# Seven quarter products for eight in the first FFN product of two half layers of a decoder step

## The chip, the cores and the metric

The kernel runs on one core of a Trainium2 chip. The metric is the device time of one execution in microseconds (us); lower is better. The core's engines are PE (TensorE, the matmuls), DVE (VectorE), ACT (ScalarE), POOL (GpSimd, which here only issues DMAs) and SP (SyncE, which issues DMAs). Each engine works through its own list of instructions in order and waits on semaphores; the lists are fixed when the program is built.

## The reference

One step of a two-layer decoder: a retention layer, then a layer with windowed attention, each followed by a feed-forward network (FFN), with a norm before and after each part. 1024 tokens of a prompt and 32 of samples go through together, D = 1024 wide, the FFN 4096 wide. What matters here is the FFN, whose square makes a plain float32 product necessary:

```python
def ffn(h, g_pre, w1, w2, g_post):
    u = jax.nn.relu(rms_norm(h, g_pre) @ w1)
    return h + rms_norm((u * u) @ w2, g_post)
```

## The kernel before

The tokens are cut into half 0 (512) and half 1 (512 and the 32 samples, 544). Activations lie with the model dimension on the 128 partitions, so a token is a column. Every float32 product is made of three products of a reduced type: a number is cut into a high part `hi` and a rest `lo`, and `passes` lists hi x hi, hi x lo and lo x hi.

The FFN runs once for each half and layer: f0 (half 0, layer 0, its first product up to 1174 us in the profile, its second to 1353), f1 (half 1, layer 0), fa (half 0, layer 1) and f2 (half 1, layer 1, from 2489 us to the end). `Ffn.up(i)` (line 739) does 256 of the 4096 columns of W1, which is called a block here: `load_w` (310) loads two tiles of 512 KB by SP into `wraw` (line 318, two buffers), ACT casts the high part (`whi`, 328), DVE subtracts for the low part (`wlo`, 329), `proj_fm` (350) does the matmuls (line 356): for each of two groups of 128 columns eight steps along D, three passes, and one piece of 512 tokens (half 0) or two of 272 (half 1). ACT applies relu and square (748, 749), and POOL stores the block to HBM (`uD`, line 751). `ups` runs the blocks, `downs` the second product with `uD` fetched back by POOL (756).

The work between the products (norms, attention, transposes) is written as generators, called sides. `tick` (174) lets the present side take a step each time the matmuls have earned one, at a rate from the table `RATES` (156); `drain` takes all steps that are left. A scheduler then orders all instructions for each engine by the order of the text and the buffers. The sides named here are `norms` (281) with its statistic in `norm_r` (251: squares on ACT, sums on DVE, then two matmuls against ones, lines 265 and 266); "f0", the norm of half 1 beside f0's first product; "at1", "smp", "wo1" and "lt1", half 1's attention, its output product and the norm after it, all beside fa's second product; "at0", "wo0" and "lt0", the same for half 0 beside f1's; and "fo", the last norm, stores and transposes of half 0's output, beside f2's first product. Tiles called `x4` (146) are 8.5 KB in each partition; there are 13. PSUM has eight banks, four `mm` and four `aux`.

Of the kernel before, what the change touches and what calls it, by code (L numbers as in the profile page):

```python
# [116 lines left out]
def body(ctx, tc,  # L117
# [11 lines left out]
    def f32(ap):  # L129
        return ap.bitcast(F32)  # L130
# [30 lines left out]
    def side(gen, rate=None):  # L161
        sides.append((gen, rate))
# [88 lines left out]
    def norm_r(get, w):  # L251
# [19 lines left out]
        V.scalar_tensor_tensor(out=t, in0=t, scalar=3.0, in1=y0, op0=ALU.subtract, op1=ALU.mult)  # L271
        return t

    def xs_alloc():
        hi, lo = [x4(), x4()], [x4(), x4()]
        return [(hi[k // 4][:, k % 4], lo[k // 4][:, k % 4]) for k in range(KT)]
# [70 lines left out]
    def passes(a, b):  # L347
        return [(a[0], b[0]), (a[0], b[1]), (a[1], b[0])]
# [383 lines left out]
    class Ffn:  # L732
# [6 lines left out]
        def up(self, i):  # L739
# [10 lines left out]
            s_ = 2 * (i % 2)  # L750
            G.dma_start(out=uD[self.half][:, 2 * i:2 * i + 2], in_=self.st[:, s_:s_ + 2, :t_])  # L751

        def fetch(self, j):
            hi, lo = x4(), x4()
            t_ = TT[self.half]
            G.dma_start(out=f32(lo)[:, :, :t_], in_=uD[self.half][:, 4 * j:4 * j + 4])
            self.parts[j] = (hi, lo)

        def cut(self, j):
            t_ = TT[self.half]  # L760
            hi, lo = (t[:, :, :t_] for t in self.parts[j])
# [450 lines left out]
            S.activation(out=sel[:, i], in_=sel[:, i], func=AF.Copy, scale=den[:, i:i + 1])  # L1212

    def swa_sides(sw, half, am=None, skr=None):
        xs = []

        def late():
            xs.extend(xs_alloc())
            yield from norms(half, sw.y, g_spost, xs=xs, pre=g_f1)

        side(sw.attend(), f"at{half}")
        if half:
            side(sw.attend_sample(am, skr), "smp")
        side(sw.wo(), f"wo{half}")
        side(late(), f"lt{half}")
        return xs

    CHUNKS = [1, 2, 2, 2, 1]
    with tc.tile_pool(name="rp", bufs=1) as rp:
        G.dma_start(out=g_first, in_=gsrcs[0].rearrange("(k p) -> p k", p=P))  # L1230
# [4 lines left out]
        rets = [Ret(0, [(hi[k // 4][:, k % 4], lo[k // 4][:, k % 4]) for k in range(KT)], rp), None]  # L1235
        for _ in range(RATES["w0"]):
            next(ini)
        first = rets[0].qk_w(0, 0)
        run(ini)
        for g in (gen, x_store(0, loads), x_store(1)):  # L1240
            side(g, "x")
        qk = rets[0].qk(0, [[(0, 256)], [(256, 256)]], first)
        drain()
        prev = None
        for half in range(2):
            r = rets[half]
            for h in range(RH):
                pace[0] = RATES["vg"][half]
                last = h == RH - 1
                vs = r.v(h)  # L1250
                if last:
                    drain()
                    prev[0].wout(*prev[1:])
                    prev = None
                    xs = xs_alloc()
                    norm = norms(1 - half, xs=xs, pre=g_f0 if half else g_rpre)
                    side(norm, "n1")
                sg = r.g(h)
                while sides and (not last or sides[0][0] is norm):
                    advance()  # L1260
                og = (x4(), x4())
                side(r.core(h, qk, vs, sg, og))
                pace[0] = RATES["core"][half]
                if prev is not None:
                    prev[0].wout(*prev[1:])
                if prev is not None and prev[1] == RH - 1:
                    side(norms(0, prev[0].y, g_rpost), "rp")
                prev = (r, h, og)
                if not last:
                    qk = r.qk(h + 1)  # L1270
                elif half == 0:
                    rets[1] = Ret(1, xs, rp)
                    qk = rets[1].qk(0)
                else:
                    f0 = Ffn(0, 0, xs)
                    pace[0] = RATES["cl"]
                    for i in range(3):
                        f0.up(i)
        drain()
        prev[0].wout(*prev[1:])  # L1280
    with tc.tile_pool(name="sp", bufs=1) as sp:
# [56 lines left out]
        finish(f2, hT)  # L1338
# [31 lines left out]
```

## Time and profile before

| what | us |
|---|---|
| median of 3 runs (2905.68 to 2906.97) | 2906.42 |
| the profiled execution | 2905.74 |
| its span (first to last instruction) | 2903.9 |
| PE busy | 2849.2 (98%) |
| DVE busy | 1526.7 (53%) |
| ACT busy | 1264.1 (44%) |
| f0, blocks 5 to 15 of the first product | 123.1 |
| f2, blocks 2 to 15 of the first product | 172.4 |

PE is the engine that the others serve, and an average over the span hides where it waits. So the time of a stretch is read from the timeline of an engine that acts once in a block (POOL, with its store), and the waits from the rows on PE that have idle time before them. In such a row the start, the duration, the line and the tiles are followed by the idle time before it and what ended it.

### The profile page before, as it was taken

Reading aid. Unit: us, or ns where it says so; the run is one execution under the profiler, and the core shown is the slowest. Engines: PE = TensorE matmul, PEld = TensorE weight load, DVE = VectorE, ACT = ScalarE, POOL = GpSimd, SP = SyncE. Lnnn points to the kernel's source line nnn. Section 1 sums busy time; section 2 is a strip of 40 time slices with the busy share of each in tenths; the row PEclk is TensorE's granted clock in tenths of the full one; section 3 lists DMA queues with packets and bytes.
Section 4 is the critical chain, followed back from the end, with each engine's and each line's share of the span. In section 5 each row is a group of like instructions: output and inputs, shape, how many; then the busy total and the mean of one; then the engine's idle time right before and its main releaser. Section 6 shows DMA issues by size and latency. Waiting matters only on the chain.

```text
span 2903.9 us, 42531 instructions
## 1 busy us (share of the span) xinstructions
PE 2849.2 (98%) x16989; PEld 2487.6 (86%) x16989; DVE 1526.7 (53%) x3045; ACT 1264.1 (44%) x2554; POOL 177.3 (6%) x262
## 2 busy tenths in 40 slices
PE   8999999999999999999999999999999999899998
PEld 7888888888989788888998898978877788899998
DVE  5444565576566644553444664654357535542345
ACT  3343353343325444432545764445458533444322
POOL 2000000011010100000000000000010100000000
PEclk9999999999999999999999999999999999899999
DMA  6322332455263645553554333355432434346432
GB/s 206 93 83 89 95 113 87 157 169 176 91 209 97 219 144 173 179 152 98 163 165 131 126 96 95 109 164 163 156 128 87 131 94 150 105 148 217 157 103 68
DMA packets 418420, 391.08 MB, mean 135 GB/s; under 512 B 13878, under 2 KB 360286, under 8 KB 416174
## 3 DMA queue, kind: packets, MB, share of 16 engines
q1 hardware_dynamic: 380191, 248.97, 29.0%
q0 software_dynamic: 36848, 137.36, 13.3%
q8 instruction: 133, 2.18, 0.3%
q10 hardware_dynamic: 1183, 2.04, 0.2%
q14 instruction: 65, 0.53, 0.1%
HBM read 308.73 MB, written 79.56 MB: 134 GB/s over the span
## 4 chain that ended last, share of the span: by engine, by line
PE 88%; issue 4%; DVE 3%; DMA 2%; ACT 2%; POOL 0%; SPq 0%; DVEq 0%; ACTq 0%; POOLq 0%
PE mm L356 66%; PE mm L496 6%; PE mm L940 5%; PE aux L629 2%; PE aux L638 2%; DMA wraw<-in_ffn_w_dram 1%; PE aux L705 1%; PE aux L1098 1%; PE aux L714 1%; PE aux L547 1%; PE aux L573 1%; PE aux L1065 1%; PE aux L496 1%; DVE wlo L329 0%; ACT whi L328 0%
## 5 line engine op out<-in xcount | busy, mean ns | idle before, releaser
L356 PE MATMUL mm<-x,whi 128*128 128x272 f32 (+2 forms) x8768 | 1912.6, 325 | 11.9 <-DVE y L367 6.0
L356 PEld LDWEIGHTS mm<-x,whi 128*128 128x128 f32 x8768 | 1381.7, 189 | 153.3 <-issue 9.8
L356 PE MATMUL mm<-x,wlo 128*128 128x272 f32 (+2 forms) x4384 | 1192.5, 324 | 0.0
L329 DVE TENSOR_TENSOR wlo<-wraw,whi 128x1024 fp32r<-128x1024 f32 x396 | 483.7, 1222 | 713.4 <-ACT whi L328 712.8
L328 ACT CAST whi<-wraw 128x1024 fp32r<-128x1024 f32 x396 | 415.4, 1049 | 938.2 <-PE mm L356 798.1
L356 PEld LDWEIGHTS mm<-x,wlo 128*128 128x128 f32 x4384 | 738.4, 189 | 62.1 <-DVE wlo L329 0.6
L367 DVE TENSOR_TENSOR y<-y,mm 128x272 f32<-128x272 f32 (+1 forms) x264 | 130.9, 516 | 182.5 <-PE mm L356 182.0
L496 PE MATMUL mm<-whi,x 128*128 128x512 f32 x512 | 166.9, 397 | 0.0
L940 PE MATMUL mm<-whi,x 128*128 128x512 f32 x384 | 124.2, 394 | 0.0
L496 PEld LDWEIGHTS mm<-whi,x 128*128 128x128 f32 x512 | 96.1, 189 | 22.8 <-DVE n L476 0.8
L496 PE MATMUL mm<-wlo,x 128*128 128x512 f32 x256 | 101.2, 395 | 0.0
L764 DVE TENSOR_TENSOR x<-x,x 128x1024 fp32r<-128x1024 f32 (+1 forms) x64 | 78.7, 1254 | 32.3 <-ACT x L763 32.1
L257 DVE TENSOR_TENSOR n<-n 128x272 f32<-128x272 f32 (+1 forms) x196 | 84.2, 430 | 10.7 <-ACT n L256 2.4
L749 ACT ACTIVATE x<-x 128x272 f32<-128x272 f32 (+1 forms) x192 | 88.5, 497 | 1.5
L940 PEld LDWEIGHTS mm<-whi,x 128*128 128x128 f32 x384 | 72.1, 188 | 17.6
L751 POOL DMA_DIRECT2D uD<-x x64 | 40.2, 628 | 746.4 <-ACT x L749 655.6
L748 ACT ACTIVATE x<-mm 128x272 f32<-128x272 f32 (+1 forms) x192 | 81.3, 457 | 3.6 <-PE mm L356 3.5
L763 ACT CAST x<-x 128x1024 fp32r<-128x1024 f32 (+1 forms) x64 | 66.8, 1076 | 22.1 <-DMA x<-uD 15.2
L940 PE MATMUL mm<-wlo,x 128*128 128x512 f32 x192 | 75.7, 394 | 0.0
L334 DVE SCALAR_TENSOR_TENSOR wlo<-wraw,gall,whi 128x512 fp32r<-128x512 f32 x48 | 34.6, 747 | 59.8 <-ACT whi L333 59.6
L496 PEld LDWEIGHTS mm<-wlo,x 128*128 128x128 f32 x256 | 48.4, 189 | 10.5
L333 ACT ACTIVATE whi<-wraw,gall 128x512 fp32r<-128x512 f32 x48 | 32.7, 717 | 54.5 <-PE aux L940 19.8
(310 smaller groups left out, 2531.8 us busy)
## 6 DMA issues: line engine op xcount, KB each, us to landing
wraw<-in_ffn_w_dram SPq DMA_DIRECT2D x256, 512.0 KB, 4.1
wraw<-in_ret_w_in_dram SPq DMA_DIRECT2D x96, 512.0 KB, 3.8
uD<-x POOLq DMA_DIRECT2D x32, 544.0 KB, 5.7
x<-uD POOLq DMA_DIRECT2D x16, 1088.0 KB, 7.4
wraw<-in_ret_w_out_dram SPq DMA_DIRECT2D x32, 512.0 KB, 3.5
x<-in_state_ret_dram SPq DMA_DIRECT2D x32, 512.0 KB, 5.3
out_dram<-x POOLq DMA_DIRECT2D x32, 512.0 KB, 3.4
uD<-x POOLq DMA_DIRECT2D x32, 512.0 KB, 5.7
```

The costliest lines, as they stand in the source:

```text
L257: V.tensor_tensor(out=acc, in0=acc, in1=sq, op=ALU.add)
L328: S.copy(out=hi, in_=raw)
L329: V.tensor_tensor(out=lo, in0=raw, in1=f32(hi), op=ALU.subtract)
L356: T.matmul(p_[:, :w], lhsT=a, rhs=b[:, o:o + w], start=(k == 0 and i == 0), stop=(k == n - 1 and i == 2))
L367: V.tensor_tensor(out=y[m][:, o:o + w], in0=y[m][:, o:o + w], in1=ps, op=ALU.add)
L496: T.matmul(ps[c][:a.shape[1]], lhsT=a, rhs=b, start=(k == 0 and i == 0), stop=(k == KT - 1 and i == len(prods) - 1))
L629: T.matmul(ps, lhsT=a, rhs=b, start=(n == 0), stop=(n == len(prods) - 1))
L748: S.activation(out=d, in_=ps, func=AF.Relu)
L749: S.activation(out=d, in_=d, func=AF.Square)
L763: S.copy(out=hi[:, a:a + 2], in_=f32(lo)[:, a:a + 2])
L764: V.tensor_tensor(out=lo[:, a:a + 2], in0=f32(lo)[:, a:a + 2], in1=f32(hi)[:, a:a + 2], op=ALU.subtract)
L940: T.matmul(ps[c][:a.shape[1]], lhsT=a, rhs=b, start=(k == 0 and i == 0), stop=(k == KT - 1 and i == len(prods) - 1))
```

## The change

In f0 the blocks 5 to 15, and in f2 the blocks 2 to 15, are computed by another scheme. Tokens are cut in two (A11 and A12 are the two halves of the model dimension for the first half of the tokens, A21 and A22 those for the second), and the block of W1 in four quarters B. Strassen's scheme in Winograd's form needs seven products of quarters for eight, with four sums of A (S1 to S4) and four of B (T1 to T4) ahead, and sums of the products behind. Each is four steps along D times three passes.

`Quarters.build` makes S1 to S4 once for a half layer, as a side ("s7") beside two ordinary blocks. `Seven` loads the raw weights of a block into an `x4` tile (two DMAs of 512 KB on SP), and a quarter of 256 KB into one of four slots of `t1`. Two sums of weights are made by DMAs on POOL that add to what lies in the buffer (T1 in `t1`, T3 in the raw tile, 256 KB each); the other two are DVE additions. `prep` casts on ACT and takes low parts on DVE. `seven` does the products in seven PSUM banks (pool p7 in place of pp) and their sums: one ACT copy and four DVE operations. Relu and square are then one ACT instruction each for the block. The sides "f0" and "fo" now run beside the second products, and their rates change, as do those of the attention sides in f1's and fa's second products.

```diff
-    RATES = {'vg': (1.445, 1.54), 'core': (1.95, 3.135), 'cl': 6.936, 'x': 1.76, 'n1': 3.38, 'rp': 1.549, 'f0': 0.43, 'nf0': 0.7, 'nf1': 0.72, 'at0': 2.4, 'wo0': 2.4, 'lt0': 2.4, 'at1': 3.25, 'smp': 3.25, 'wo1': 3.25, 'lt1': 3.25, 'fo': 0.43, 'warm': 8, 'w0': 5}
+    RATES = {'vg': (1.445, 1.54), 'core': (1.95, 3.135), 'cl': 6.936, 'x': 1.76, 'n1': 3.38, 'rp': 1.549, 'f0': 0.9, 's7': 1.25, 'nf0': 0.7, 'nf1': 0.72, 'at0': 2.6, 'wo0': 2.6, 'lt0': 2.6, 'at1': 3.8, 'smp': 3.8, 'wo1': 3.8, 'lt1': 3.8, 'fo': 0.9, 'warm': 8, 'w0': 5}
...
+    class Quarters:
...
+        def build(self):
...
+            diff(r0, "A22", "A21")
+            yield
+            minus(r1, r0, "A11")
+            yield
+            cut("S1", r0)
+            yield
+            minus(r0, r1, "A12")
+            cut("S2", r1)
+            yield
+            diff(r1, "A11", "A21")
+            yield
+            cut("S4", r0)
+            cut("S3", r1)
+            yield
...
+    class Seven:
+        def __init__(self, src, t1):
+            self.t1 = t1.rearrange("p (k c) -> p k c", k=4)
+            self.raw = x4(F32).rearrange("p a b -> p (a b)")[:, :2048].rearrange("p (i k c) -> p i k c", i=2, k=8)
+            for i in range(2):
+                nc.sync.dma_start(out=self.raw[:, i], in_=src[:, i * P:(i + 1) * P].rearrange("(k p) c -> p k c", p=P))
+                if i == 0:
+                    nc.sync.dma_start(out=self.t1, in_=src[:512, :P].rearrange("(k p) c -> p k c", p=P))
+            G.dma_start(out=self.t1, in_=src[:512, P:].rearrange("(k p) c -> p k c", p=P), accum_op=ALU.add)
+            G.dma_start(out=self.raw[:, 1, 0:4], in_=src[512:, P:].rearrange("(k p) c -> p k c", p=P), accum_op=ALU.add)
...
+        def prep(self):
...
+            S.copy(out=ha, in_=raw[:, 0])
+            h2, l2 = quarter("B22")
+            S.copy(out=h2, in_=b22)
+            low(ha, la, raw[:, 0])
+            low(h2, l2, b22)
+            h1, l1 = quarter("T1")
+            S.copy(out=h1, in_=self.t1)
+            add(b22, self.t1, b22)
+            hb, lb = pair()
+            S.copy(out=hb, in_=raw[:, 1])
+            add(b21, b22, b21)
+            low(h1, l1, self.t1)
+            h4, l4 = quarter("T4")
+            S.copy(out=h4, in_=b21)
+            low(hb, lb, raw[:, 1])
+            low(h4, l4, b21)
...
+    def seven(xq, wq, after):
...
+        prod(p1, "A11", "B11")
+        u1 = c[:, 3, :s]
+        S.copy(out=u1, in_=p1)
+        prod(px[:, 1], "S2", "T2")
+        prod(px[:, 0], "A12", "B21")
+        V.tensor_tensor(out=slot(0), in0=twice(u1), in1=px, op=ALU.add)
+        u2 = c[:, 0, s:2 * s]
+        prod(py[:, 1], "S3", "T3")
+        prod(py[:, 2], "S1", "T1")
+        V.tensor_tensor(out=slot(1), in0=twice(u2), in1=py[:, 1:3], op=ALU.add)
+        u3, v = c[:, 1, :s], c[:, 1, s:2 * s]
+        prod(py[:, 0], "S4", "B22")
+        V.scalar_tensor_tensor(out=slot(2), in0=twice(v), scalar=-1.0, in1=py[:, 0:2], op0=ALU.mult, op1=ALU.subtract)
+        prod(p4, "A22", "T4")
+        V.tensor_tensor(out=u2, in0=u3, in1=p4, op=ALU.add)
+        return c
...
+        def ups7(self, a, b):
+            self.xq = Quarters(self.half, self.xs)
+            side(self.xq.build(), "s7")
...
+            self.up(a - 2)
+            w = [load(a)]
+            self.up(a - 1)
+            drain()
+            run(w[0].prep())
+            w.append(load(a + 1))
+            bank_pool("p7")
+            for i in range(a, b):
+                if i + 2 < b:
+                    w.append(load(i + 2))
+                if i == b - 2:
+                    self.fetch(0)
+                self.up7(i, w[i - a], w[i + 1 - a] if i + 1 < b else None)
+            bank_pool("pp")
...
+        f0.ups7(5, 2 * NFB)
         xs = xs_alloc()
         side(norms(1, rets[1].y, g_rpost, xs=xs, pre=g_f0), "f0")
-        f0.ups(3, 2 * NFB)
         f0.downs(CHUNKS)
...
-        f2.ups(0, 1)
+        f2.ups7(2, 2 * NFB)
         side(norms(0, fa.y, g_fp1, spill=False, keep=True), "fo")
...
-        f2.ups(1, 2 * NFB)
         f2.downs([2, 2, 2, 1])
```

The scheduler's order at three places follows, as far as the prediction speaks of them. In the rows a number behind a name is a buffer's.

POOL, late in f0's first product. Before, its list there has the stores of blocks (line 751), two fetches for the second product (756) and a load for the norm (286):

```order
L751 DMA uD0_98<-x4_10258 128x2x512 x2
L286 DMA x4_10481<-hD1_97 128x8x272
L756 DMA x4_10592<-uD0_98 128x4x512
L751 DMA uD0_98<-x4_10428 128x2x512
L756 DMA x4_10622<-uD0_98 128x4x512
```

Of the change, POOL in the middle of f0's seven-product blocks (line 940 is the store, 359 adds to a raw tile, 358 to a slot of t1):

```order
L940 DMA uD0_98<-x4_9751 128x2x512
L359 DMA x4_9991<-in_ffn_w1_dram 128x4x128
L358 DMA x4_9544<-in_ffn_w1_dram 128x4x128
L940 DMA uD0_98<-x4_9876 128x2x512
L359 DMA x4_10116<-in_ffn_w1_dram 128x4x128
L358 DMA x4_9544<-in_ffn_w1_dram 128x4x128
L940 DMA uD0_98<-x4_10001 128x2x512
```

Between the stores of two blocks (tiles 9751 and 9876) there now stand two accumulating DMAs of later blocks. SP loads the raw tile 9991 of the block four later into the place of 9751, so behind the first of these stores.

DVE in the same blocks. Before, it has two low parts of weights for each block and a part of the norm beside them; of the change, one block reads (375 are low parts, 378 the sums of weights, 440 to 449 the sums of products):

```order
L440 TENSOR_TENSOR x4_10251<-x4_10251,px_10248 128x512
L375 TENSOR_TENSOR wlo_10327<-x4_10116,whi_10326 128x1024
L375 TENSOR_TENSOR wlo_10390<-x4_10241,whi_10389 128x1024
L375 TENSOR_TENSOR y_10311<-x4_9544,y_10310 128x512
L444 TENSOR_TENSOR x4_10251<-x4_10251,py_10249 128x512
L375 TENSOR_TENSOR y_10345<-x4_10116,y_10344 128x512
L449 TENSOR_TENSOR x4_10251<-x4_10251,p4_10250 128x256
L447 SCALAR_TENSOR_TENSOR x4_10251<-x4_10251,py_10249 128x512
L375 TENSOR_TENSOR y_10406<-x4_10241,y_10405 128x512
L378 TENSOR_TENSOR x4_10241<-x4_9544,x4_10241 128x512
L378 TENSOR_TENSOR x4_10241<-x4_10241 128x512
```

The low parts of the next block (from 10116) and of the one after it (from 10241) now stand between this block's sums, and the sums of weights of a block stand two blocks ahead of their use. PE does a block's products in the order p1 (its first six matmuls), py0 of the block before, the rest of p1, px, py1 and py2, p4.

PE at the end of fa's second product. Before, the norm's last statistic (265, 266) comes behind 24 matmuls of f2's first block (tiles 22305 to 22308 are f2's input):

```order
L356 MATMUL mm<-x_22308,whi 128x272
L356 MATMUL mm<-x_22306,wlo 128x272
L265 MATMUL aux<-n,onesd 128x272
L266 MATMUL aux<-n,onesd 128x272
L356 MATMUL mm<-x_22305,whi 128x272 x3
```

Of the change (272 and 273 are the statistic, 22800 and 22801 a piece of the second product's input, 22874 on f2's):

```order
L530 MATMUL mm<-x_22800,wlo 128x512
L272 MATMUL aux<-n,onesd 128x272
L530 MATMUL mm<-x_22800,whi 128x512
L530 MATMUL mm<-x_22801,whi 128x512
L273 MATMUL aux<-n,onesd 128x272
L530 MATMUL mm<-x_22800,wlo 128x512
```

It now stands within the second product, with 13 of its matmuls behind it, and 85 matmuls behind the statistic before it.

## Rows read from the trace of the kernel before

**Rows 1.** The page, parts 1 and 4: busy time; the chain by line.

```profile
PE 2849.2 (98%) x16989; PEld 2487.6 (86%) x16989; DVE 1526.7 (53%) x3045; ACT 1264.1 (44%) x2554; POOL 177.3 (6%) x262
...
PE mm L356 66%; PE mm L496 6%; PE mm L940 5%; PE aux L629 2%; PE aux L638 2%; DMA wraw<-in_ffn_w_dram 1%; PE aux L705 1%; PE aux L1098 1%; PE aux L714 1%; PE aux L547 1%; PE aux L573 1%; PE aux L1065 1%; PE aux L496 1%; DVE wlo L329 0%; ACT whi L328 0%
```

**Rows 2.** Timeline of POOL: start, us, engine, line, operation, [idle before <-releaser].

```profile
1039.86 0.73 POOL L751 DMA_DIRECT2D uD<-x  x1 [34.96 <-ACT x L749]
1050.92 0.71 POOL L751 DMA_DIRECT2D uD<-x  x1 [10.32 <-ACT x L749]
...
1174.03 0.71 POOL L751 DMA_DIRECT2D uD<-x  x1 [4.17 <-ACT x L749]
...
2515.63 0.54 POOL L751 DMA_DIRECT2D uD<-x  x1 [11.43 <-ACT x L749]
2527.66 0.53 POOL L751 DMA_DIRECT2D uD<-x  x1 [11.49 <-ACT x L749]
...
2688.07 0.55 POOL L751 DMA_DIRECT2D uD<-x  x1 [11.95 <-ACT x L749]
```

**Rows 3.** Windows of both stretches: length, PE, PEld, DVE, ACT, POOL, clock, DMA share, GB/s.

```profile
1050.92:1174.03 123.11, 123.11 (x533) 99.52 (x533) 53.28 (x80) 62.39 (x99) 11.94 (x17) 1.00 0.58 183
2515.63:2688.07 172.44, 172.44 (x1383) 172.44 (x1382) 56.43 (x78) 75.31 (x163) 10.50 (x19) 1.00 0.54 175
```

**Rows 4.** Timeline of PE, matmuls of 256 columns early in the kernel.

```profile
28.56 0.40 PE L356 MATMUL mm<-x,whi 128*128 128x256 f32 x2
...
28.91 0.42 PE L356 MATMUL mm<-x,whi 128*128 128x256 f32 x2
```

**Rows 5.** Groups by form: busy, mean ns | idle before; line 505's min/median/max ns.

```profile
L329 DVE TENSOR_TENSOR wlo<-wraw,whi 128x1024 fp32r<-128x1024 f32 x24 | 29.4, 1224 | 68.1 <-ACT whi L328 68.1
L328 ACT CAST whi<-wraw 128x1024 fp32r<-128x1024 f32 x23 | 24.1, 1050 | 57.7 <-PE mm L356 57.5
...
L764 DVE TENSOR_TENSOR x<-x,x 128x1088 fp32r<-128x1088 f32 x4 | 5.0, 1288 | 2.0 <-ACT x L763 2.0
...
L505 DVE TENSOR_TENSOR x<-mm,y x32: 677/692/694, 79.7 to 883.1; 128x512 fp32r<-128x512 f32 x32
```

**Rows 6.** f0's stores (line 751), landing of two 512 KB loads (701, us), the page.

```profile
L751 POOL DMA_DIRECT2D uD<-x x12: 707/716/719, 1050.9 to 1174.0; - x12
...
DMA to landing us min/median/max: 3.6/5.6/6.5
...
DMA to landing us min/median/max: 4.3/4.7/5.2
...
hD<-x POOLq DMA_DIRECT2D x16, 256.0 KB, 3.9
```

**Rows 7.** End of fa.downs: PE's timeline, windows, the chain; last PE's waits, 1000 to 2460.

```profile
2468.30 0.60 PE L265 MATMUL aux<-n,onesd 128*128 128x272 f32 x1 [3.86 <-ACT n L261]
...
2485.17 0.59 PE L265 MATMUL aux<-n,onesd 128*128 128x272 f32 x1 [8.89 <-ACT n L261]
...
2489.23 1.27 PE L356 MATMUL mm<-x,whi 128*128 128x272 f32 x4 [2.99 <-ACT x L305]
...
2468.30:2470.80 2.50, 2.50 (x6) 2.06 (x7) 1.84 (x3) 0.00 (x0) 0.00 (x0) 0.50 0.09 25
...
2485.00:2489.00 4.00, 1.07 (x2) 0.58 (x2) 2.54 (x6) 0.84 (x3) 0.00 (x0) 0.50 0.62 169
2489.00:2496.00 7.00, 6.77 (x32) 6.77 (x33) 6.72 (x18) 4.63 (x13) 0.00 (x0) 0.55 0.01 2
...
2459.74 7.07 DMA wraw<-in_ffn_w_dram
...
2468.90 2.13 PE mm L356 x5
...
2489.23 10.89 PE mm L356 x63
...
PE mm L356 <- DVE y L367: 5.6, 2, 3.9
```

More of the change, by code (lines that the diff above doesn't have):

```diff
@@ L272, in norm_r, with __init__, fill @@
         return t
-    def xs_alloc():
-        hi, lo = [x4(), x4()], [x4(), x4()]
-        return [(hi[k // 4][:, k % 4], lo[k // 4][:, k % 4]) for k in range(KT)]
+    class Parts(list):
+        def __init__(self, hi=None, lo=None):
+            if hi:
+                self.fill(hi, lo)
+        def fill(self, hi, lo):
+            self.extend((hi[k // 4][:, k % 4], lo[k // 4][:, k % 4]) for k in range(KT))
+            self.hi, self.lo = hi, lo
+    def xs_alloc():
+        return Parts([x4(), x4()], [x4(), x4()])
@@ new lines, in body, with pair, quarter, low @@
+    class Seven:
[8 more added lines that the diff above has]
+            G.dma_start(out=self.raw[:, 1, 0:4], in_=src[512:, P:].rearrange("(k p) c -> p k c", p=P), accum_op=ALU.add)
+            self.f = {}
+        def prep(self):
+            raw, f = self.raw, self.f
+            b11, b21, b12, b22 = raw[:, 0, 0:4], raw[:, 0, 4:8], raw[:, 1, 0:4], raw[:, 1, 4:8]
+            def pair():
+                return [wp.tile([P, 1024], F32R, tag=g, bufs=WB, name=g).rearrange("p (k c) -> p k c", k=8)
+                        for g in ("whi", "wlo")]
+            def quarter(n):
+                f[n] = [yt(TM, F32R)[:, :512].rearrange("p (k c) -> p k c", k=4) for _ in range(2)]
+                return f[n]
+            def low(h, l, r):
+                V.tensor_tensor(out=l, in0=r, in1=f32(h), op=ALU.subtract)
+            def add(r, a, b):
+                V.tensor_tensor(out=r, in0=a, in1=b, op=ALU.add)
+            ha, la = pair()
+            f["B11"], f["B21"] = (ha[:, 0:4], la[:, 0:4]), (ha[:, 4:8], la[:, 4:8])
+            S.copy(out=ha, in_=raw[:, 0])
+            yield
+            h2, l2 = quarter("B22")
+            S.copy(out=h2, in_=b22)
+            low(ha, la, raw[:, 0])
+            yield
+            low(h2, l2, b22)
+            yield
+            h1, l1 = quarter("T1")
+            S.copy(out=h1, in_=self.t1)
+            add(b22, self.t1, b22)
+            yield
+            hb, lb = pair()
+            f["T3"], f["T2"] = (hb[:, 0:4], lb[:, 0:4]), (hb[:, 4:8], lb[:, 4:8])
+            S.copy(out=hb, in_=raw[:, 1])
+            add(b21, b22, b21)
+            low(h1, l1, self.t1)
+            yield
+            h4, l4 = quarter("T4")
+            S.copy(out=h4, in_=b21)
+            low(hb, lb, raw[:, 1])
+            yield
+            low(h4, l4, b21)
+            yield
+        def rows(self, n):
+            h, l = self.f[n]
+            return [(h[:, k], l[:, k]) for k in range(4)]
@@ new lines, in seven, with slot, twice, prod @@
+    def seven(xq, wq, after):
+        s = xq.s
+        pool = banks[1]
+        p1 = pool.tile([P, 512], F32, tag="p1", name="p1")[:, :s]
+        px = pool.tile([P, 2, 512], F32, tag="px", name="px")[:, :, :s]
+        py = pool.tile([P, 3, 512], F32, tag="py", name="py")[:, :, :s]
+        p4 = pool.tile([P, 512], F32, tag="p4", name="p4")[:, :s]
+        c = x4(F32)
+        def slot(i):
+            return c[:, i, :2 * s].rearrange("p (a t) -> p a t", a=2)
+        def twice(ap):
+            return ap.unsqueeze(1).to_broadcast([P, 2, s])
+        def prod(ps, a, b):
+            A, B = xq.rows(a), wq.rows(b)
+            for k in range(4):
+                for i, (w_, x_) in enumerate(passes(B[k], A[k])):
+                    T.matmul(ps, lhsT=w_, rhs=x_, start=k == 0 and i == 0, stop=k == 3 and i == 2)
+            after()
+        prod(p1, "A11", "B11")
[14 more added lines that the diff above has]
+        return c
@@ L751, in up, with up7, after, load @@
             G.dma_start(out=uD[self.half][:, 2 * i:2 * i + 2], in_=self.st[:, s_:s_ + 2, :t_])
+        def up7(self, i, wq, nxt):
+            t_ = TT[self.half]
+            steps = nxt.prep() if nxt else iter(())
+            def after():
+                next(steps, None)
+            c = seven(self.xq, wq, after)
+            run(steps)
+            d = c.rearrange("p (a b) t -> p a b t", b=2)[:, :, 0, :t_]
+            S.activation(out=d, in_=d, func=AF.Relu)
+            S.activation(out=d, in_=d, func=AF.Square)
+            G.dma_start(out=uD[self.half][:, 2 * i:2 * i + 2], in_=d)
+        def ups7(self, a, b):
+            self.xq = Quarters(self.half, self.xs)
+            side(self.xq.build(), "s7")
+            t1 = x4(F32)
+            def load(i):
+                return Seven(ffn_w1[self.l][:, i * 256:(i + 1) * 256], t1[:, i % 4, :512])
+            self.up(a - 2)
[11 more added lines that the diff above has]
+                self.up7(i, w[i - a], w[i + 1 - a] if i + 1 < b else None)
+            bank_pool("pp")
+            self.cut(0)
+            self.xq = None
         def fetch(self, j):
@@ L1234, in body @@
         loads = next(ini)
-        rets = [Ret(0, [(hi[k // 4][:, k % 4], lo[k // 4][:, k % 4]) for k in range(KT)], rp), None]
+        rets = [Ret(0, Parts(hi, lo), rp), None]
         for _ in range(RATES["w0"]):
```

42 lines of the change are left out of this document (37 added, 5 removed).

## The prediction

> **What bounds the kernel now.** I read the page's first line first: TensorE (PE) is busy 98% of the span, and the chain of work that ended last is 66% matmuls of line 356 [rows 1]. So time is saved only by fewer matmul columns or by removing PE's idle time. Then the two stretches that the change rewrites. The stores of one 256-column block of the first FFN product follow each other on POOL; their spacing is the time of a block [rows 2]. In f0 (half 0, layer 0) the eleven blocks i=5 to 15 take 1174.03 - 1050.92 = 123.1 us, 11.19 each; an undisturbed one takes 1050.92 - 1039.86 = 11.06, for 48 matmuls of 512 columns, 0.230 each. In f2 (half 1, layer 1) the fourteen blocks i=2 to 15 take 2688.07 - 2515.63 = 172.4 us, 12.32 each; an undisturbed one 12.03, for 96 matmuls of 272, 0.1253 each. PE is busy throughout both, at clock 1.00, and the DMA engines are already at 0.58 and 0.54 of their time there [rows 3]. Last the waits of PE: the largest lie together at the end of fa.downs.
>
> The profiled execution took 2905.74 us (span 2903.9); the median of the runs is 2906.42, so 0.7 us is added at the end.
>
> **Matmuls removed.** A block becomes seven quarter products of 4 x 3 matmuls: 84 of 256 columns (half 0) or 272 (half 1). Three 256-column matmuls start 28.91 - 28.56 = 0.35 us apart [rows 4], 0.118 each, each with its own weights. By PE alone a block is 84 x 0.118 = 9.9 and 84 x 0.1253 = 10.5 us.
>
> PE alone does not set the pace. In the new order each block holds a loop: px ends, ACT casts hb (1.05), DVE does hb's low part and the next block's ha (2 x 1.22), T1's low part (at most 0.69, the price of a 512-wide operation) and slot 1 (0.69) [rows 5], then PE does py0 (12), the rest of p1 (6) and px (24): 42 matmuls, 4.97 us. With six handovers of some 0.1 that is 10.4 us in half 0; in half 1 (43 matmuls, 5.4 us, slot 1 544 wide) 10.95. DVE as a whole has 2 x 1.22 + 8 x 0.69 + 0.45 = 8.4 us of work per block, so it keeps up, without much room. Gain: 11 x (11.19 - 10.4) = 8.7 and 14 x (12.32 - 10.95) = 19.2: **-27.9**. Of that the matmuls of the moved sides (f0's norm, fo's norm, stores and token transposes) come back in the downs: 11 x (11.19 - 11.06) + 14 x (12.32 - 12.03) = **+5.5**. Their DVE and ACT work lies beside matmuls of the downs in both places and costs nothing while those engines stand near half load; if that cover were gone it would be waits of up to 3.9 us, as PE has at an end of downs today [rows 7].
>
> **Entering and leaving.** Quarters.build has 14 DVE operations of 1024 or 1088 elements, 1.22 to 1.29 each [rows 5], 18 us in f2; with the lows of two ordinary blocks (4 x 1.22) and the first prep (5.9) that makes 28.8 us of DVE, starting some 6 us after f2's first matmul, as the last normed columns come then. It ends near 34.5 us; PE asks for the last sum after two ordinary blocks (24.1) and three products (4.7), near 29. So a stall of 5.5 us. In f0 the input is ready early, and only 2 us of DVE backlog remain. Each switch of the PSUM pool waits for the last reader, about 1 us, four times. Sum 2 + 5.5 + 4 = 11.5, rounded with a short half-clock stretch to **+12** (bounds 6 and 18).
>
> **The new loop over POOL and SP.** Four pairs of buffers serve raw weights and results, so the load of raw(b+4) waits until store(b) has landed. On POOL the queue is in the order store(b), accumulate of raw(b+4), accumulate of a t1, store(b+1): the first accumulate waits for the load, and behind it stands store(b+1), though its data are long done; the load of raw(b+5) waits for that. Before, POOL held only stores here, and loads waited for DVE. A lap T is: store landing L + landing of the two raw loads A + two issues on POOL. A store lands in 3.6 us at the least, 5.6 in the median beside loads; a pair of 512 KB loads, issued 0.4 us apart, has its second landing at 5.2, so A = 5.6; an issue takes 0.71 [rows 6]. T = 10.6 to 12.6. The trace has no accumulating DMA: from below it costs what a plain 256 KB store does (3.9 to land, no more in the lap than its issue), from above it holds the store behind it as long as two more transfers would, some 1.4 us, T = 14; a gain is excluded, since it adds traffic. I take L = 5.0, nearer to the median, as the two accumulates are in flight with every store: **T = 12.0**, above both block times. The first accumulate is wanted by DVE's add some two blocks after the store: about 4 us to spare. Six laps in f0 and nine in f2 then give 6 x (12.0 - 10.4) - 4 = 5.6 and 9 x (12.0 - 10.95) - 4 = 5.4: **+11** (bounds 0 at T = 10.6, and 17.6 + 23.5 = 41 at T = 14).
>
> **The end of fa.downs.** Here PE waits 3.86, 8.89 and 2.99 us in the 21 us to 2489 [rows 7]: the norm's last statistics (line 265) come after all matmuls of the downs and 24 of f2, and DVE needs some 17 us from one statistic to the next (2485.17 - 2468.30 = 16.9). After 8.89 us idle the clock is 0.50 for 4 us and 0.55 over the next 7; 63 matmuls take 10.89 there, against 63 x 0.1253 = 7.9. So 8.9 + 3.0 + 3.0 = 14.9 can be had, and 3.9 + 1 more if the first wait goes too; that one hangs on a weight load of 7.07 us. With rates of 3.8 for 3.25 all four statistics lie within the downs, the last with 13 matmuls of 512 and 24 of 272 behind it: 3.0 + 3.0 us over a chain of 3 us from it to the first normed columns. The last two stand 85 matmuls (19.6 us) apart, over DVE's 17. I take **-13**; bounds -4 (if the faster pace makes PE wait within the attention) and -19. At the end of f1.downs (2.4 to 2.6) PE waits 3.9 us once; **-1** (bounds -4 and +2).
>
> **Sum.** -27.9 + 5.5 + 12 + 11 - 13 - 1 = -13.4. 2905.74 - 13.4 = 2892.3, and 0.7 to the median: **2893**.
>
> **Rivals.** (a) *The queue loop rules.* The accumulates hold the stores, T = 14. Then +41 for +11: 2923; at T = 13.5 it is 15 + 19 = 34, 2916. It decides from T = 12.9 on (11 + 12 = 24, no gain left). For it: the DMA engines above half load before anything is added, and store medians of 5.6. Against: stores that land in 3.6. (b) *The queue loop is free*, T at most 11: 2882; with the smaller costs at the ends 2876. For it: the POOL queue carries little today. "DMA: Bandwidth & Descriptors" of the Trainium skill (Anatomy of one DMA, SWDGE path) fits 2.0 us plus bytes over 436e3 for a DMA of POOL, an estimate of 3.2 us for the store; the sum by it would be this rival's. The trace differs: 5.6 in the median. (c) *The change of rates gives nothing* in fa.downs, because DVE falls behind at the faster pace and the last statistic waits as before: 2905. (d) *PE idles in every lap and loses its clock.* After 3.86 us idle the clock was 0.50 for the next 2.5 us [rows 7]. At that level five 512-column matmuls took 2.13 us, 0.21 per 256 columns, a block 17.9 us; fifteen laps so would be 15 x 6 = 90 us more, 2983. In a lap that waits 1 to 2 us on the queue, a short slow stretch lies within the wait and adds nothing; I hold it unlikely. "TensorE: Matmul & The Clock Gate" (HAM oscillation) of the Trainium skill tells of a kernel that waited for a DMA in each tile and started every tile at half clock; no row here shows it for waits this short.
>
> **How the numbers follow.** Forecast (T from 11.3 to 12.7) 0.45, 2885 to 2901; (b) 0.20; (a) 0.23; (c) 0.10; (d) 0.02. Range 2876 to 2920: from (b) with small costs to T near 13.8; some 0.16 is left out. A measurement of this kernel can tell 0.2%, 5.8 us, from no change. Faster, below 2900.6: the forecast but its upper edge, and (b): 0.60. Same: that edge, (c), and T near 13: 0.16. Slower, above 2912.2: most of (a), and (d): 0.24.
>
> **What would show it.** Stores of f0's blocks spaced 10.4 us at first and near 12 later, f2's 10.95, then 12: the loop as forecast. Even spacing of 10.4 and 10.95 to the end would be (b), 13 to 14 (a). The POOL rows should show accumulates waiting for loads and SP's loads waiting for stores; PE's waits should be named after DVE's adds or the low parts. The waits of line 265's successor of 8.89 and 3.86 should be gone, with the clock near 1.00 up to f2; a stall of some 5 us should stand at f2's first seven-product block. If blocks are longer than 11 us with the DMAs on time, the DVE loop was under-priced, and the step on handovers is wrong.

## The result and the profile after

The changed kernel takes 3004.98 us (2999.66 to 3010.87), the kernel before 2906.05 in the same measurements: a ratio of 1.0343, interval 1.0321 to 1.0365. It is slower by 99 us, where 2893 us was forecast. The time went to the two stretches that the change rewrites. Times in the table are differences between stores of the profiled executions, as in [rows 2].

| stretch | before | after | difference |
|---|---|---|---|
| f0, stores of blocks 4 to 15 | 123.1 | 157.2 | +34.1 |
| from there to f1's first store | 190.9 | 190.7 | -0.2 |
| f1's last store to fa's first (f1.downs, attention of half 0) | 373.0 | 377.6 | +4.6 |
| fa's last store to f2's first (fa.downs, attention of half 1) | 416.3 | 394.2 | -22.1 |
| f2, stores of blocks 0 to 15 | 184.4 | 257.5 | +73.1 |
| from there to the end | 215.9 | 219.5 | +3.6 |

The differences add up to 93 us, as the profiled execution after took 2999.66 us.

The first page of the profile after, parts 1 and 4, which answer to [rows 1]:

```profile
PE 2853.3 (95%) x17217; PEld 2508.9 (84%) x17217; DVE 1697.7 (57%) x3298; ACT 1314.3 (44%) x2556; POOL 245.6 (8%) x312
...
PE 74%; issue 9%; DMA 8%; DVE 5%; ACT 2%; POOL 2%; SPq 0%; POOLq 0%; DVEq 0%; ACTq 0%
```

PE has fewer columns to do and is yet as long busy as before (2853 us against 2849), at a lower granted clock (0.974 for 0.990 over the whole), and the chain has fallen from 88% PE to 74%, with DMA and issue in its place. PE's longest wait is now a new one, for slot 1 of the sums of products (line 444); in each row stand the total, the number of waits and the longest:

```profile
PE py L432 <- DVE x L444: 85.9, 18, 9.2
PE px L432 <- ACT whi L396: 9.6, 2, 8.0
```

DVE's line 444 is cheap; it stands behind low parts of weights that have not landed. The timeline of POOL in f0, which answers to [rows 2], shows why (359 adds into a raw tile, 358 into a slot of t1, 940 is the store):

```profile
1081.95 1.28 POOL L359 DMA_DIRECT2D x<-in_ffn_w_dram  x1 [10.41 <-DMA x<-in_ffn_w_dram]
1087.18 1.29 POOL L358 DMA_DIRECT2D x<-in_ffn_w_dram  x1 [3.95 <-DVE y L375]
1087.93 1.28 POOL L940 DMA_DIRECT2D uD<-x  x1
1099.89 1.27 POOL L359 DMA_DIRECT2D x<-in_ffn_w_dram  x1 [10.68 <-DMA x<-in_ffn_w_dram]
1104.64 1.27 POOL L358 DMA_DIRECT2D x<-in_ffn_w_dram  x1 [3.48 <-issue]
1105.40 1.26 POOL L940 DMA_DIRECT2D uD<-x  x1
```

From one store to the next it is 1105.40 - 1087.93 = 17.5 us. The first accumulate waits 10.7 us for loads that waited for the store; the second starts 4.75 us after the first, although it waits for nothing the profile shows ("issue"); the store follows 0.75 us later. (The row at 1087.18 names DVE's line 375, which had ended 0.6 us before; the accumulate ahead had landed 0.3 us before.) That the loads wait for the store stands in the waits of SP from 1060 to 1140 us:

```profile
SPq L355 <- DMA uD<-x: 58.3, 4, 15.3
```

Lines of the chain of waits through this lap and the next, in order of time, give the pieces. Between the second and the third line the chain as the profile follows it runs over ACT, DVE and PE, which is taken up under the clock below:

```profile
1087.93 5.20 DMA uD<-x
...
1093.25 4.15 DMA x<-in_ffn_w_dram
...
1110.96 5.32 DMA x<-in_ffn_w_dram
...
1116.95 1.29 POOL x L359
1118.24 3.26 issue
...
1121.55 0.72 POOL x L358
1122.26 5.42 DMA uD<-x
```

A lap is 5.2 to 5.4 us for the store, 6 for the raw loads, 0.7 until the accumulate's issue, 1.3 + 3.3 to 3.5 until the next accumulate, 0.75 until the store. A store of line 940 lands in 5.2 us in the median, an accumulate in 4.6:

```profile
DMA to landing us min/median/max: 3.2/5.2/7.1
...
x<-in_ffn_w_dram POOLq DMA_DIRECT2D x50, 256.0 KB, 4.6
```

The second accumulate starts about 0.3 us after the first has landed. So the place of the loss was known; what makes an accumulate wait for the one ahead of it was not.

### The profile page after: what moved, and what is told of

It reads as the page before. It is cut to its first block, busy times and chain, and to the rows that moved or that the text cites. A ratio compares the mean times of both kernels' runs of the same rounds, so it can differ in the third digit from the quotient of the medians.

```text
span 2997.8 us, 43583 instructions
## 1 busy us (share of the span) xinstructions
PE 2853.3 (95%) x17217; PEld 2508.9 (84%) x17217; DVE 1697.7 (57%) x3298; ACT 1314.3 (44%) x2556; POOL 245.6 (8%) x312
## 3 DMA queue, kind: packets, MB, share of 16 engines
q0 software_dynamic: 63248, 150.47, 16.5%
## 4 chain that ended last, share of the span: by engine, by line
PE 74%; issue 9%; DMA 8%; DVE 5%; ACT 2%; POOL 2%; SPq 0%; POOLq 0%; DVEq 0%; ACTq 0%
PE mm L530 51%; PE mm L670 6%; PE mm L1156 4%; DMA x<-in_ffn_w_dram 4%; DMA uD<-x 3%; PE aux L803 2%; PE aux L812 1%; PE py L432 1%; PE aux L879 1%; DVE wlo L503 1%; PE aux L1314 1%; PE px L432 1%; POOL x L358 1%; POOL x L359 1%; DMA x<-uD 1%
## 5 line engine op out<-in xcount | busy, mean ns | idle before, releaser
L530 PE MATMUL mm<-x,whi 128*128 128x272 f32 (+2 forms) x7520 | 1653.5, 326 | 11.5 <-DVE y L541 6.2
L530 PEld LDWEIGHTS mm<-x,whi 128*128 128x128 f32 x7520 | 1189.7, 189 | 137.2 <-issue 10.2
L530 PE MATMUL mm<-x,wlo 128*128 128x272 f32 (+2 forms) x3760 | 1030.8, 325 | 0.6 <-DVE wlo L503 0.5
L503 DVE TENSOR_TENSOR wlo<-wraw,whi 128x1024 fp32r<-128x1024 f32 x346 | 422.9, 1224 | 474.3 <-ACT whi L502 472.1
L530 PEld LDWEIGHTS mm<-x,wlo 128*128 128x128 f32 x3760 | 635.2, 189 | 55.6 <-DVE wlo L503 1.5
L432 PE MATMUL py<-x,y 128*128 128x272 f32 (+1 forms) x600 | 103.2, 332 | 85.9 <-DVE x L444 85.9
L432 PEld LDWEIGHTS py<-x,y 128*128 128x128 f32 x600 | 94.3, 230 | 90.6 <-DVE x L444 90.1
L375 DVE TENSOR_TENSOR wlo<-x,whi 128x1024 fp32r<-128x1024 f32 x50 | 61.2, 1225 | 120.2 <-ACT whi L382 93.5
L432 PE MATMUL px<-x,whi 128*128 128x272 f32 (+1 forms) x400 | 79.5, 298 | 9.6 <-ACT whi L396 9.6
L432 PEld LDWEIGHTS px<-x,whi 128*128 128x128 f32 x400 | 67.0, 202 | 10.1 <-ACT whi L396 10.1
```

Of the source, the lines that this page charges most:

```text
L375: V.tensor_tensor(out=l, in0=r, in1=f32(h), op=ALU.subtract)
L432: T.matmul(ps, lhsT=w_, rhs=x_, start=k == 0 and i == 0, stop=k == 3 and i == 2)
L503: V.tensor_tensor(out=lo, in0=raw, in1=f32(hi), op=ALU.subtract)
L530: T.matmul(p_[:, :w], lhsT=a, rhs=b[:, o:o + w], start=(k == 0 and i == 0), stop=(k == n - 1 and i == 2))
```

## Experiments

Theory one: POOL's queue of DMAs has room for a limited number of packets, an accumulate takes many, and two don't fit; so the second holds the queue, and the store behind it. The rivals: an accumulate waits for the one ahead whatever its size; the loads themselves are too slow; the loop over PE and DVE is longer than priced. Where no ratio stands beside a time, it is that of one execution.

**The rates alone.** The kernel before, with this edit:

```diff
-'at0': 2.4, 'wo0': 2.4, 'lt0': 2.4, 'at1': 3.25, 'smp': 3.25, 'wo1': 3.25, 'lt1': 3.25
+'at0': 2.6, 'wo0': 2.6, 'lt0': 2.6, 'at1': 3.8, 'smp': 3.8, 'wo1': 3.8, 'lt1': 3.8
```

> The kernel before with one edit: the rates of the attention sides as in the change (2.6 for 2.4 beside f1's second product, 3.8 for 3.25 beside fa's). In the traces of before and after, the stretch from fa's last ups to f2's first store is 21.7 us shorter, and the stretch across f1's downs 4.7 us longer. Theory: these two come from the rates alone; so 2906 - 17 = 2889 here. Rival: they come from the moved sides or from other loads, and the rates alone give less than 5 us: 2901 or more.

Measured: 2894.26 us, ratio 0.9971 (0.9960 to 0.9981). By the profile f1.downs is 3.5 us longer, and fa.downs 15.4 shorter, of the 22.1 that the changed kernel gained there. The rates make most of that gain and the whole is smaller than expected; where the other 6.6 us come from was not taken apart. What PE waited for between 2400 and 2530 us is now

```profile
PE mm L356 <- ACT x L305: 1.8, 1, 1.8
PE mm L356 <- DVE wlo L329: 0.8, 1, 0.8
```

in place of the 3.86, 8.89 and 2.99 us of [rows 7].

**Plain copies for accumulates.** In the changed kernel:

```diff
-...rearrange("(k p) c -> p k c", p=P), accum_op=ALU.add)
+...rearrange("(k p) c -> p k c", p=P))
```

> The changed kernel with the two accumulating DMAs of a block made plain copies of the same shape, in the same places; the sums T1 and T3 are so left out. Theory: an accumulating DMA that follows another on POOL waits until that one has landed, 4.7 us each, and this is 4.7 us of a lap of 17.5. Without it a lap is 5.2 (store) + 5.9 (loads) + 1.5 = 12.6 us: stores of blocks 12 to 13 us apart, 2910 to 2930 in all. Rival: it is the number of pieces (512 of 512 bytes) that fills the queue, whether they accumulate or not: laps of 17 us and 2990 to 3005 as before. Second rival, the time of the loads themselves: laps of 15 or more.

Measured: 2904.28 us. POOL's timeline at the same place:

```profile
1089.07 0.77 POOL L359 DMA_DIRECT2D x<-in_ffn_w_dram  x1 [11.58 <-DMA x<-in_ffn_w_dram]
1089.83 0.76 POOL L358 DMA_DIRECT2D x<-in_ffn_w_dram  x1
1090.58 0.71 POOL L940 DMA_DIRECT2D uD<-x  x1
1101.62 0.77 POOL L359 DMA_DIRECT2D x<-in_ffn_w_dram  x1 [10.32 <-DMA x<-in_ffn_w_dram]
```

The second copy follows the first by 0.76 us. Laps are 12.5 us in f0 (1152.4 - 1065.1 over seven) and 12.7 in f2, as expected; the whole is 6 us under the range expected. So 101 us of the changed kernel hang on the accumulates. The number of pieces alone (512 for both) does not fill the queue; but the packets differ. All DMAs of POOL, before, after, and here (packets, MB, share):

```profile
q0 software_dynamic: 36848, 137.36, 13.3%
```

```profile
q0 software_dynamic: 63248, 150.47, 16.5%
```

```profile
q0 software_dynamic: 40848, 150.47, 15.0%
```

Fifty accumulates add 63248 - 36848 = 26400 packets, 528 each; fifty copies of the same shape and bytes add 4000, 80 each. The number of packets and the accumulating itself are so still mixed, which the wide rows and the scratch space below take apart.

**Stores on ACT.** In the changed kernel:

```diff
-            G.dma_start(out=uD[self.half][:, 2 * i:2 * i + 2], in_=d)
+            nc.scalar.dma_start(out=uD[self.half][:, 2 * i:2 * i + 2], in_=d)
```

> The changed kernel with the stores of the seven-product blocks issued by ACT, behind their square, so that no store stands behind an accumulating DMA. Theory: the lap over store, load and accumulate is broken; POOL still has two accumulates of 4.9 us for each block, 9.8, under the 10.4 and 10.95 of the loop over PE and DVE. Blocks 10.4 to 11.2 us apart, f0's blocks 5 to 15 near 122 us for 157, f2's near 185 for 258, 2890 to 2905 in all. Rival: the DMA engines are too full, or the loop over DVE and PE is longer than 12 us; then blocks stay above 13 us, 2940 or more.

Measured: 2908.95 us. f0's stretch is 122.1 us, as expected, and f2's blocks are 10.9 us apart once they run (2566.0 to 2653.3, eight). f2's whole stretch is 191 us for the 185 expected, as its second, third and fourth store came 30.2, 16.6 and 14.0 us after the one before: seven accumulates, 5 to 10 us apart, stand on POOL there before the third, five of them ahead of the second ordinary block's store. POOL in f2 now goes by accumulates alone, 5.2 to 6.6 us apart:

```profile
2578.76 1.29 POOL L358 DMA_DIRECT2D x<-in_ffn_w_dram  x1 [4.82 <-issue]
2584.27 1.28 POOL L359 DMA_DIRECT2D x<-in_ffn_w_dram  x1 [4.22 <-DVE x L447]
2589.45 1.29 POOL L358 DMA_DIRECT2D x<-in_ffn_w_dram  x1 [3.90 <-issue]
2596.05 1.28 POOL L359 DMA_DIRECT2D x<-in_ffn_w_dram  x1 [5.31 <-DVE x L449]
```

Two rows name DVE, but each accumulate here starts 0.3 us after the one ahead has landed. So it is the store behind the accumulates that closes the loop, and without it two of them in a block just fit. The DMA engines are not too full for blocks of 10.9 us.

**All sums on DVE.** In the changed kernel:

```diff
-                if i == 0:
-                    nc.sync.dma_start(out=self.t1, in_=src[:512, :P].rearrange("(k p) c -> p k c", p=P))
-            G.dma_start(out=self.t1, in_=src[:512, P:].rearrange("(k p) c -> p k c", p=P), accum_op=ALU.add)
-            G.dma_start(out=self.raw[:, 1, 0:4], in_=src[512:, P:].rearrange("(k p) c -> p k c", p=P), accum_op=ALU.add)
...
+            add(self.t1, b11, b12)
+            add(b12, b12, b22)
             h1, l1 = quarter("T1")
```

> The changed kernel with all four sums of weights on DVE, from the raw tile: neither accumulating DMAs nor loads of a third quarter. DVE has 2 x 0.69 us more for each block, 9.8 us in all. Theory: with POOL's queue free, the loop over PE and DVE sets the pace, 10.6 to 11.5 us for a block, also at f2's start: f0's stretch near 123 us, f2's near 165; 2875 to 2895 in all. Rival: DVE becomes the bound, with blocks of 12 us or more: 2905 to 2925.

Measured: 2879.58 us, ratio 0.9920 (0.9905 to 0.9935): faster than both kernels. Six blocks of f0 take 1150.3 - 1088.6 = 61.7 us, 10.28 each; thirteen of f2 take 2658.9 - 2520.4 = 138.5, 10.65 each. The windows of f0 (1100 to 1150) and f2 (2521 to 2660), with the clock and the DMA share last but two and last but one:

```profile
1100.00:1150.00 50.00, 49.56 (x410) 48.60 (x410) 43.04 (x63) 30.79 (x39) 3.69 (x5) 1.00 0.52 159
```

```profile
2521.00:2660.00 139.00, 137.50 (x1080) 136.07 (x1079) 112.50 (x159) 82.78 (x103) 11.86 (x18) 1.00 0.52 164
```

PE is busy 99% of both. DVE at 86% and 81% is near its end but not the bound. So PE by itself now all but sets the pace: the blocks are 0.4 and 0.15 us longer than the 9.9 and 10.5 priced for PE alone. In the changed kernel the same 50 us of f0 read

```profile
1100.00:1150.00 50.00, 36.23 (x252) 35.60 (x252) 22.40 (x32) 16.82 (x22) 9.83 (x9) 0.81 0.60 135
```

What is left is at f2's start: PE waited 7.0 us once for the cast of the first weights, behind the sums of activations on DVE.

**One accumulate for two.** In the changed kernel:

```diff
-            G.dma_start(out=self.raw[:, 1, 0:4], in_=src[512:, P:].rearrange("(k p) c -> p k c", p=P), accum_op=ALU.add)
...
+            add(b12, b12, b22)
             h1, l1 = quarter("T1")
```

> The changed kernel with one of the two accumulating DMAs of a block (T3, into the raw tile) made a DVE addition; T1 still comes by an accumulating DMA. So POOL's queue holds one accumulate between two stores, no two in a row. Theory: an accumulate makes only the next accumulate wait for its landing, not a plain store behind it; the lap is then store 5.2, loads up to the third quarter's 6.0, one issue 1.3, 12.5 us: as with plain copies (blocks 11.2 to 13.8), 2895 to 2915 in all. Rival: an accumulate holds whatever follows on POOL: laps of 16 to 17 us, 2960 or more.

Measured: 2940.8 us. The time lies between both expectations, and the laps decide: 13.7 us in f0 (five from 1064.5 to 1132.8), 13.9 in f2. A store behind one accumulate goes out 0.8 us after it:

```profile
1090.66 1.30 POOL L358 DMA_DIRECT2D x<-in_ffn_w_dram  x1 [12.17 <-DVE x L377]
1091.46 1.23 POOL L940 DMA_DIRECT2D uD<-x  x1
1104.08 1.31 POOL L358 DMA_DIRECT2D x<-in_ffn_w_dram  x1 [11.38 <-DVE x L377]
1104.88 1.24 POOL L940 DMA_DIRECT2D uD<-x  x1
```

So the rival falls: an accumulate does not hold whatever follows. My lap of 12.5 was too short by 1.2: the accumulate waits for the third load, which lands 6.6 to 7.3 us after the first was issued, and 0.7 us more pass until its issue (the rows name DVE's line 377, but this 0.7 us is the same in each lap).

**The rate beside f1's second product, back at 2.4.** In the kernel with all sums on DVE, `at0`, `wo0` and `lt0` 2.4 for 2.6.

> The kernel with all sums on DVE, with the rate beside f1's second product back at 2.4. The stretch across f1's downs was 3.5 to 4.6 us longer wherever the rate was 2.6. Theory: the rate did that; 2880 - 4 = 2876. Rival: the longer stretch comes from elsewhere and stays: 2880.

Measured: 2879.83 us, ratio 0.9921 (0.9905 to 0.9938); the stretch is 378.2 us, with 2.6 it was 377.0. The theory is not borne out. But the next run has the same order of PE's work up to there, and its stretch is 375.4: two executions of the same work differ by 2.8 us, so one profile each cannot settle a difference of 4.

**A third ordinary block ahead of f2's.** In the kernel just shown:

```diff
-            self.up(a - 2)
+            for j in range(a - lead, a - 1):
+                self.up(j)
...
-        f2.ups7(2, 2 * NFB)
+        f2.ups7(3, 2 * NFB, 3)
```

> The last kernel, with three ordinary blocks in place of two ahead of f2's seven-product blocks (13 of these for 14). With two, the first seven-product block there took 24.3 us for 10.65: PE waited for ACT's cast, behind a chain of DVE work (the sums of activations and of weights) that ended 6.8 us after PE had come. Theory: a third ordinary block (12.0 us) covers that chain: the stall of 13.7 us falls to 2 to 5, and one block more at 12.0 for 10.65 costs 1.4; 2876 - 8 = 2868 (2864 to 2871). Rival: the chain spreads with the longer cover, or the stall comes from loads that wait for stores: 2875 to 2879.

Measured: 2874.16 us, ratio 0.9905 (0.9891 to 0.9920), the fastest here. The first seven-product block follows its forerunner by 2519.92 - 2504.90 = 15.0 us for 24.3, and PE's longest wait there is 0.7 us. f2's stretch is 167.9 us for 175.5, but its first store came 3.9 us later behind fa's last (398.7 for 394.8), with no PE wait above 0.7 us. The mechanism is right; 5.7 us were gained for the 8 expected.

**Accumulates of wide rows.** In the changed kernel both accumulates read `ffn_w1[l][:128, c:c + 512]`, with c = 256 min(i, 14):

```diff
-            G.dma_start(out=self.t1, in_=src[:512, P:].rearrange("(k p) c -> p k c", p=P), accum_op=ALU.add)
+            G.dma_start(out=self.t1.rearrange("p k c -> p (k c)"), in_=wide, accum_op=ALU.add)
```

> The changed kernel with both accumulating DMAs reading another part of W1, in rows of 2 KB (128 pieces) in place of 512 bytes (512 pieces), the same 256 KB into the same places; the sums T1 and T3 are so other sums. In the traces an accumulate of 512-byte pieces made 528 packets and the plain copy in its place 80. Theory one: POOL's queue has room for a limited number of packets, and two accumulates of 528 do not fit; if the wide rows bring the packets near 144 the wait of 4 us between two accumulates goes, laps of 13 to 14 us, 2915 to 2945 in all. Theory two: an accumulate waits for the one ahead whatever its pieces: laps of 17 us, near 3000. If the packets stay at 528, both expect 3000, and the run tells nothing between them.

Measured: 2928.17 us. All DMAs of POOL, then its timeline in f0:

```profile
q0 software_dynamic: 44048, 150.47, 15.9%
```

```profile
1091.11 0.84 POOL L359 DMA_DIRECT2D x<-in_ffn_w_dram  x1 [12.02 <-DMA x<-in_ffn_w_dram]
1091.85 0.97 POOL L358 DMA_DIRECT2D x<-in_ffn_w_dram  x1
1092.57 1.00 POOL L940 DMA_DIRECT2D uD<-x  x1
```

An accumulate is now 144 packets (7200 more over fifty), and the next one follows in 0.74 us. They still accumulate, so theory two falls. Laps are 14.0 us in f0. An accumulate does not land sooner: 4.9 us in the median for 4.6, with two now in flight at once.

**More scratch space.** In the changed kernel, in the call that builds the program:

```diff
-dynamic_dma_scratch_size=2048
+dynamic_dma_scratch_size=3072
```

> The changed kernel with one number changed: the scratch space for POOL's DMAs is 3072 bytes in each partition for 2048. The engines' lists of instructions stay the same. Theory one (room for packets): a half more room holds two accumulates at once, the 4 us between the two go, laps fall from 17.5 to 13 to 14 us, 2915 to 2945 in all. Theory two (an accumulate waits for the one ahead by itself): nothing changes, laps of 17.5, 2995 to 3010.

Measured: 2956.71 us, ratio 1.0188 (1.0156 to 1.0221). POOL in f0, where the packets are still 528 for each accumulate:

```profile
1095.70 1.28 POOL L359 DMA_DIRECT2D x<-in_ffn_w_dram  x1 [12.47 <-DMA x<-in_ffn_w_dram]
1096.48 1.81 POOL L358 DMA_DIRECT2D x<-in_ffn_w_dram  x1
1097.23 1.79 POOL L940 DMA_DIRECT2D uD<-x  x1
```

The hold of 4 us is gone by one number, with every engine's list unchanged: it is room in the scratch space that the second accumulate waits for. The profile has nothing that names this wait; it shows it as "issue". On the ring of descriptors "DMA: Bandwidth & Descriptors" of the Trainium skill (SWDGE vs HWDGE vs iDMA) says that POOL writes each DMA's descriptors into rings in SBUF, from which the DMA engines drain them. It does not say what happens when there is no room; this run shows it. Laps are 14.5 and 14.9 us, a little over the 13 to 14 expected, and the time is 12 us above the expected range: the store now goes out with both accumulates in flight and lands in 5.9 us in the median, up to 8.5.

f1.downs took 385 us in this run and 384 in the next, for 373 to 380 in all others, and the traces tell most of it. POOL stores 1 MB of a norm there (line 471) and then loads 1 MB for the next (460). These are plain DMAs. With 2048 bytes, then with 3072:

```profile
1881.29 0.86 POOL L471 DMA_DIRECT2D hD<-x  x1 [37.81 <-DVE n L264]
1887.47 0.89 POOL L460 DMA_DIRECT2D x<-hD  x1 [5.31 <-ACT n L268]
```

```profile
1865.74 0.86 POOL L471 DMA_DIRECT2D hD<-x  x1 [38.03 <-DVE n L264]
1866.59 0.89 POOL L460 DMA_DIRECT2D x<-hD  x1
```

With 2048 the load, too, was held until 0.3 us after the store had landed (1887.16). With 3072 it goes out at once, and a load of weights issued 1.5 us later takes 10.2 us, where the two before it took 3.6. DVE's low part waits for these weights, line 541 stands behind it on DVE, and PE waits 12.7 us for that line in place of 6.2:

```profile
1868.13 10.19 DMA wraw<-in_ffn_w_dram
...
PE mm L530 <- DVE y L541: 12.7, 3, 8.1
```

```profile
PE mm L530 <- DVE y L541: 6.2, 3, 3.2
```

So the room counts for plain DMAs too, and a hold is not always a loss.

What the room is counted in stays open. It is not packets alone: by the traces' records each of these two plain DMAs makes 272, and the pair, 544, did not go out together with 2048 bytes, while an accumulate and the store behind it, 528 + 144, did in the run with one accumulate.

**Both.** The scratch space of 3072 with the stores on ACT.

> The changed kernel with 3072 bytes of that scratch space and with the stores of the seven-product blocks on ACT. Theory one: neither the accumulates hold each other nor do stores stand behind them; blocks 10.2 to 11 us, no burst of waiting accumulates at f2's start, 2880 to 2892. Theory two: as with the stores on ACT alone, 2909.

Measured: 2906.34 us, ratio 1.0012 (1.0001 to 1.0024). f2's blocks are 10.5 us apart from 2554 on, but for three of 11.4, 11.6 and 15.4, and its whole stretch is 181 us for 191 with the smaller space. So most blocks do as theory one says; but f2's second, third and fourth store still came 19.9, 15.0 and 13.1 us after the one before, f1.downs is 3 to 11 us longer than in the runs with 2048, for the reason just shown, and the stretch from f2's last store to the end is 228 us for 215 to 222. The whole is not in the expected range.

## Why the prediction failed

**The matmuls and the loop over PE and DVE** came out near: 10.4 and 10.95 us for a block were forecast, 10.28 and 10.65 measured with the queue free. That is partly luck. The forecast had the loop over PE and DVE set the pace, with 0.5 us over PE alone; in those blocks PE is busy 99% of the time, and from 1088 to 1150 us it waits 0.3 us in all for DVE. The side work that moves to the downs was +5.5 in the sum; the two stretches behind f0 and f2 changed by -0.2 and +3.6.

**The loop over POOL and SP** is the step that failed. Its path was named as it is: store, raw load, accumulate, accumulate, store, and rival (a), "the queue loop rules", is what happened. But the lap was taken as 12.0 and bounded at 14, and it is 17.5. With plain copies it is 12.5, so without the accumulates the term would have stood (2904 us). What failed is the price of the accumulates in the lap: no more than their issue, and "from above it holds the store behind it as long as two more transfers would, some 1.4 us". Two don't fit in the queue's scratch space, and the second waits 4 us, until the first has landed. Most of the other 1.0 us over the lap with plain copies is the store's landing among accumulates, 5.2 against 4.5.

The trace before had no accumulate, but it had the hold, on plain DMAs. In f1.downs a store of a norm's rows (line 297) is followed by a load that is held (286); behind them stands the landing of the store:

```profile
1887.01 0.86 POOL L297 DMA_DIRECT2D hD<-x  x1 [26.49 <-DVE n L257]
1893.45 0.90 POOL L286 DMA_DIRECT2D x<-hD  x1 [5.58 <-issue]
...
DMA to landing us min/median/max: 6.1/6.1/6.1
```

The load starts 0.3 us after the store has landed (1887.01 + 6.1 = 1893.1), and its 5.58 us of idle time are put down to "issue". It does not need the store: the same pair went out 0.85 us apart with 3072 bytes. Rows like this one were a reason for a wider bound; the prediction took its prices from DMAs that were not held. By my own formula a lap of 17.5 gives 6 x 7.1 - 4 = 39 us in f0, and the stretch is 36.9 us longer than with the sums on DVE. For f2 it gives 9 x (17.9 - 10.95) - 4 = 58.5, and 82.7 is measured. From block 2's store on the difference is 57.5, as the formula says; the other 25 lie ahead of that store, where ten accumulates stand, five of them ahead of ordinary block 1's store. The step put this start at nothing.

**Entering and leaving**, +12: with the sums on DVE f0's first three blocks cost 38.3 - 3 x 10.28 = 7.5 us and f2's first 24.3 - 10.65 = 13.7, 21 in all, beyond the bound of 18 (in a kernel with two more DVE sums in each block). That DVE's chain ends after PE has come was right; it ended later.

**The end of fa.downs**, -13: right in mechanism, and larger, -22.1, beyond its bound of -19, with -15.4 from the rates alone. **The end of f1.downs**, -1: wrong in sign, +4.6. PE is busy 3.5 us longer there with the same matmuls (367.3 us for 363.7, clock 0.99 for 1.00), and waits 1.0 us more. The rate of 2.4 did not bring it back, and two executions differ by 2.8 us, so its cause stays open.

**The clock**, rival (d): it did fall, to 0.81 in f0's laps. After a wait of 7.34 us twelve matmuls took 2.93 us for 12 x 0.118 = 1.42:

```profile
1101.04 2.93 PE L432 MATMUL py<-x,y 128*128 128x256 f32 x12 [7.34 <-DVE x L444]
```

But the lap hardly grew by it: the next raw load went out 0.15 us after the store had landed (1105.40 + 4.99 = 1110.39, and 1110.54), as it did 0.12 and 0.14 us after the stores of the laps on either side. It also waits for DVE's low part behind these matmuls, which ended at 1110.50, so the slow path was just about as long as the one over the DMAs.

Two slips in the sums change nothing: T = 12.9 gives 11 + 13.5, and rival (c) 2906. Rival (a) had 0.23 of the chances, and the range ended at T near 13.8. A first use of an operation deserved a wider bound than the rows of a plain DMA.

## What to carry to other kernels

A DMA that adds is not a copy that adds: it takes more of its queue's room, so look at what stands behind it there, and keep a store off the queue where accumulates wait for loads. Idle time called "issue" on the engine of a queue, that ends 0.3 us after the DMA ahead has landed, is a sign of a queue without room, whatever the DMA. If a loop of buffers runs through a queue, write down its lap as a sum of landings and issues, and ask for each new kind of DMA what happens when the one ahead of it hasn't landed. The cheapest sum is the one on the engine that has the data at hand: two adds of 0.69 us on DVE replaced three DMAs for each block, and turned 99 us lost into 24 gained, 28 with one more ordinary block for cover.

## What the hardware showed

An accumulating DMA of 256 KB in rows of 512 bytes makes 528 packets and lands in 4.6 us in the median; the plain copy makes 80 and lands in 3.6. With rows of 2 KB the accumulate makes 144 and lands in 4.9, two in flight at once. With 2048 bytes of scratch space a second accumulate of 528 packets starts 0.3 us after the first has landed, with 3072 bytes 0.78 us after the first has started. A plain load of 1 MB behind a plain store of 1 MB is held in the same way with 2048 bytes and not with 3072. The profile has no name for this wait: it shows it as "issue", or names an instruction that had ended before.
